# Four reorderings on the vector and scalar engines of a streaming encoder: the norm's reciprocal, the unit copies, a join, and the priority of two sums

## The chip, the cores and the metric

One Trainium2 chip, one core of it. The time is the device time of one launch in microseconds (us). A core has a matrix engine (TensorE, PE in the rows, with its weight loads as PEld), VectorE (DVE), ScalarE (ACT), GpSimd (POOL) and SyncE (SP); POOL and SP issue the transfers here. The products of TensorE collect in banks of PSUM, which VectorE and ScalarE read out in this kernel.

## The reference

Two layers over 512 prompt rows and 8 x 16 sample rows (640 columns in the kernel), width 1024, in float32. Of each layer:

```
x += 1/2 * SwiGLU_1(RMSNorm(x))                      w_gu: 1024 -> 2 x 2816, w_down: 2816 -> 1024
h  = RMSNorm(x)
z  = h @ w_in      columns: conv B | C | V | q | k | v | gates
y_c = B * causal_depthwise_conv3(C * V)              512 channels
y_a = chunk-band attention, 8 heads x 64
m  = sigmoid(g_c) * (y_c @ w_conv_out) + sigmoid(g_a) * (y_a @ w_attn_out);  x += m @ w_o
x += 1/2 * SwiGLU_2(RMSNorm(x))
```

and a last RMSNorm. Keys, values and the convolution's state are outputs too.

## The kernel before, in words

Activations stand with the width on the partitions: 8 tiles `x` of 128 x 640. Every product is made in three parts: an operand is split into a rounded high part (`hi`, a cast on ScalarE) and the rest (`lo`, a subtraction on VectorE), and TensorE multiplies hi·hi, hi·lo and lo·hi. So each weight slab of 128 x 1024 comes in by SyncE as `raw` (3 buffers), is cast to `whi` by ScalarE (L305) and gives `wlo` on VectorE (L310); 3 buffers each.

Most products use seven multiplications of half blocks in place of eight (`seven`, `gate_up`, `down_rows`, `gate_pair`, `unit`): the 640 columns stand as two halves of 320, and sums of weights and of operands are formed ahead. Their names are X11, X21, XN6, XT5, XT7, X22, XT4, and they are made in that order, 12 matmuls of 128 x 320 each. Products collect in three banks `pa`, `pb`, `pc` (in a unit two pairs, `A` and `B`, and `C`): `pa` takes X11, then XN6 on top, XT7 on top, XT4 on top; after each step a copy or a sum reads the bank out before the next step adds to it. Four slabs (s0 to s3) feed one such group; for a group of kind `gu` VectorE also makes the weight sum `s65` (lines 270 and 271, two half sums, recorded as L249 like every `add`), for kind `mix` the sum `s6`.

How the slabs come: `slabs` is the list of all weights in order of use. `load` issues the transfer, `source` makes a slab's sum, `prep` calls `source` and casts, and puts the lo part into `pending`; `flush` issues the pending lo parts. `slab` takes the next slab and prepares the one two places on; `quiet` takes it and prepares nothing; `ahead` calls `source` for the slab after the prepared ones.

Three engines keep the order that the code is written in within blocks called `manual_schedule` (PE, DVE and ACT); in the middle of a feed-forward only PE does (from the gate after `free`), and a scheduler orders DVE and ACT there. `soon()` gives what stands inside it a higher priority with that scheduler.

The places that the change touches:

- `gate_up`, branch `first` (L756 on): the first gate of a feed-forward. Where the norm is `new` (three feed-forwards: b of layer 0, a and b of layer 1) it makes, between the products, the sum of squares (`ex.total`, five matmuls into `nps`), the root on ScalarE (`ex.root`, L585), the weight sum (`source`), the reciprocal (L589) and a diagonal of it in `ssum` (L482) by `ex.diagonal`, and spreads it over the partitions by four matmuls `nbc` (L595). Then comes XT4 into `pa`.
- `gate_up`, the other branch: the gates after it. `add(g, pa, c5)` empties `pa` ahead of XT4, `add(u, pc, u2)` empties `pc`. `add` is L249.
- `unit` (L1411 on) multiplies 8 tiles of y by 4 x 8 blocks of `w_conv_out` (`co`, twice: m0 = 0 and 4) or `w_attn_out` (`ao`, twice). After XT4 a scalar copy reads `A` out (L1435). The two units of a kind use the same two banks, with A and B exchanged.
- The table `at(place, i, jobs)` in `outputs` says which jobs are done at which spot of which gate pair or unit: `scale` and `bend` (a gate's norm and its sigmoid, L1132), `weigh`, `join` (products with the gates, L1309), `give` and `gave` (hi and lo part of the merged m, L1497 and L1504).
- Behind the last unit, `ao4`, come the products `po` with `w_o` (L372), in `mixer`: `po` 0 and `po` 1 use the banks of the unit, `po` 2 two halves `po_2a` and `po_2b`, and each has a slab of its own.

Of the kernel before, what the change touches and what calls it, by code (L numbers as in the profile page):

```python
# [10 lines left out]
F32 = mybir.dt.float32  # L11
# [169 lines left out]
def trunk(ctx: ExitStack, tc: tile.TileContext, xin, wst, small, pbias, samplebias, kcache, vcache,  # L181
# [66 lines left out]
    def add(out, a, b):  # L248
        DVE.tensor_tensor(out=out, in0=a, in1=b, op=ALU.add)  # L249
# [2 lines left out]
    whole = slice(0, CH)  # L252
    sources = {}

    def source(i):

        if i >= len(slabs):
            return None
        if i not in sources:
            kind, n, arg = slabs[i]  # L260
            ra = load(n)
            if kind == "plain":
                sources[i] = [(ra, slice(0, arg))]
            elif arg == 0:
                sources[i] = [(ra, whole)]
            else:
                rb = load(n + 1)
                if arg == 1 and kind == "gu":
                    st = sums[n] = pool[0].tile([P, CH], F32, tag="s65", name=f"s65_{n}", bufs=1)
                    add(st[:, h2], rb[:, h1], rb[:, h2])  # L270
                    add(st[:, h1], st[:, h2], ra[:, h1])
                    sources[i] = [(st, whole)]
                elif arg == 1:

                    flush()
                    st = sums[n] = spool[0].tile([P, CH // 2], F32, tag="s6", name=f"s6_{n}", bufs=1)
                    add(ra[:, h1], ra[:, h1], rb[:, h1])
                    add(st, ra[:, h1], rb[:, h2])
                    add(rb[:, h1], rb[:, h1], rb[:, h2])
                    sources[i] = [(st, h1), (rb, h1)]  # L280
                elif arg == 2:
                    if kind == "gu":
                        add(ra[:, h1], ra[:, h1], rb[:, h1])
                    add(ra[:, h2], sums.pop(n)[:, h1], ra[:, h2])
                    sources[i] = [(ra, whole)]
                else:
                    sources[i] = [(rb, h2)]
        return sources[i]
# [26 lines left out]
    def slab(hold=False):  # L315

        flush()
        i = used[0]
        used[0] += 1
        while len(ready) < min(i + 2, len(slabs)):  # L320
            prep(len(ready))
            flush()
        prep(i + 2)
        if not hold:
            flush()
        return ready[i], slabs[i]
# [414 lines left out]
    def gate_up(fp, n, ex, first, tails, put, j, pair, later, at):  # L741

        pa, pb, pc = (att(f"p{i}{n}")[:, :HT] for i in "abc")

        def mul(ps, s, half, x, ks, start, stop):
            block(ps, s, half, lambda kp: tuple(z[:, x] for z in ex.ops[kp]), ks, start, stop)

        def spot(name):
            step(later, f"g{at}{name}")

        every, most, end = range(NP), range(NP - 1), range(NP - 1, NP)
        g, u = tmp(f"g{n}"), tmp(f"u{n}")
        t1, t2 = slice(0, HT), slice(HT, T)
        c1, u2, c5 = u[:, t1], u[:, t2], g[:, t2]
        rho = ex.rho
        if first:  # L756

            new = not ex.known
            s0, s1 = quiet(), quiet()
            mul(pa, s0, 0, X11, every, True, True)  # L760
            ACT.copy(c1, pa)
            if ex.rest:
                ex.rest()
            prep(used[0])
            flush()
            for t in tails[:2]:
                t()
            mul(pc, s1, 1, XT5, every, True, True)
            ACT.copy(c5, pc)
            if new:  # L770
                ACT.activation(ex.sq, x[KT - 1], AF.Square)
                ex.add()
                mul(pb, s0, 1, X21, most, True, True)
                mul(pa, s1, 0, XN6, most, False, True)
                mul(pb, s0, 1, X21, end, True, True)
                mul(pa, s1, 0, XN6, end, False, True)
            else:
                mul(pa, s1, 0, XN6, every, False, True)
                mul(pb, s0, 1, X21, every, True, True)
            ACT.copy(u2, pa)  # L780
            add(u[:, t1], pb, c1)
            for t in tails[2:]:
                t()
            tails.clear()
            s2 = quiet()
            prep(len(ready))
            flush()

            def third():
                mul(pc, s2, 1, X22, every, False, True)  # L790
                add(u[:, t2], pc, u2)

            if new:
                third()
                ex.total(acc(f"nps{n}")[:, 0])
                ex.root()
                source(len(ready) + 1)
                ex.diagonal()
                prep(len(ready))
            mul(pa, s2, 0, XT7, every, False, True)  # L800
            add(g[:, t2], pa, c5)
            flush()
            if new:
                nbc = acc(f"nbc{n}")
                ex.spread([nbc[:, a, :HT] for a in range(2)])
            DVE.tensor_tensor(out=g[:, t2], in0=g[:, t2], in1=rho[:, t2], op=ALU.mult)
            if not new:
                third()
                prep(len(ready))
                flush()  # L810
            s3 = slab(True)[0]
        else:
            s0 = quiet()
            mul(pa, s0, 0, X11, every, True, True)
            with soon():
                ACT.copy(c1, pa)
            prep(used[0] + 1)
            spot("e1")
            held = [t() for t in tails]
            tails.clear()  # L820
            spot("e2")
            flush()
            mul(pb, s0, 1, X21, every, True, True)
            s1 = slab(True)[0]
            flush()
            mul(pa, s1, 0, XN6, every, False, True)
            with soon():
                ACT.copy(u2, pa)
            cb = fp.tile([P, 2, HT], F32, tag="cap", name=f"cb{n}", bufs=5)[:, 0]
            ACT.copy(cb, pb)  # L830
            POOL.dma_start(u[:, t1], cb, accum_op=ALU.add)
            for t in held:
                t()
            spot("e3")
            mul(pc, s1, 1, XT5, every, True, True)
            with soon():
                ACT.copy(c5, pc)
            s2 = slab(True)[0]
            spot("e4")
            mul(pa, s2, 0, XT7, every, False, True)  # L840
            add(g[:, t2], pa, c5)
            DVE.tensor_tensor(out=g[:, t2], in0=g[:, t2], in1=rho[:, t2], op=ALU.mult)
            flush()
            ahead()
            mul(pc, s2, 1, X22, every, False, True)
            add(u[:, t2], pc, u2)
            s3 = slab(True)[0]
            ahead()
        mul(pa, s3, 0, XT4, every, False, True)
        DVE.tensor_tensor(out=g[:, t1], in0=pa, in1=rho[:, t1], op=ALU.mult)  # L850
        if first:
            ahead()
        ACT.activation(g, g, AF.Silu, scale=-1.0)
        spot("e7")
        flush()

        def tail(weights=True):

            if weights:
                begin()  # L860
            DVE.tensor_tensor(out=g, in0=g, in1=rho, op=ALU.mult)
            hi = hp.tile([P, T], F32R, tag="hhi", name=f"ahi{n}")
            lo = hp.tile([P, T], F32R, tag="hlo", name=f"alo{n}")
            if pair:
                parts = pair.product(n, u, g, hi, lo)
            else:
                DVE.tensor_tensor(out=u, in0=u, in1=g, op=ALU.mult)
                parts = lambda: split(hi, lo, u)
            flush()
            if weights:  # L870
                ahead()
            else:
                parts()
            put(j, (hi, lo))
            return parts

        tails.append(tail)
# [409 lines left out]
    def outputs(l, gp, X, st, cs, yc, yas, sigmoid, gates):  # L1287
# [123 lines left out]
        def unit(name, m0, to, last=False):  # L1411
# [53 lines left out]
                add(rows(0, t2)[:, i], C[i], rows(0, t2)[:, i])  # L1465
            if last:
                add(rows(1, t2), rows(1, t2), z)
            s3 = slab(True)[0]
            ahead()
            mul(a, s3, 0, XT4, False)  # L1470
            copy(rows(1, t1), -1.0)
            flush()
            spot(me, 5)

        def weigh(*ms):
            def job():
# [42 lines left out]
        at("co0", 1, scale(4))  # L1519
        at("co0", 2, bend(4))  # L1520
        at("co0", 3, scale(6))
        at("co0", 5, bend(6))
        at("co4", 2, weigh(0, 1))
        at("co4", 5, weigh(2, 3))
        at("g8", 1, second.opening)
        at("g8", 2, second.firsts)
        at("g8", 3, second.raw_low(0))
# [7 lines left out]
        at("g12", 3, scale(10))  # L1535
        at("g12", 4, bend(8))
        at("ao0", 3, scale(12))
        at("ao0", 5, bend(10), join(0))
        at("g14", 1, join(2))
        at("g14", 2, join(1))  # L1540
        at("g14", 3, join(3))
# [1 line left out]
        at("ao4", 2, give(0, 1))  # L1543
        at("ao4", 3, gave(0, 1))
        at("ao4", 4, give(2, 3))
        at("ao4", 5, gave(2, 3))
        for m in (2, 4, 6):
            gate_pair(m)

# [576 lines left out]
```

## Time and profile before

| | |
|---|---|
| three runs | 2495.89, 2496.51, 2498.94 us, median 2496.51 |
| the profiled execution | 2496.66 us, its span 2494.7 us |
| granted clock of TensorE, mean | 0.998 |
| ScalarE busy | 1450.0 us, 58% |
| VectorE busy | 2119.2 us, 85% |
| transferred | 308.10 MB, mean 124 GB/s |

The page has the busy time of each engine, then the waits. A row of the timeline reads: start in us from the beginning of the span, length in us, engine, line of the kernel, operation, output<-inputs by the program's names, sizes, number, and in brackets the idle time ahead of it with what ended it. Matmuls overlap: one begins every 0.147 us and its record is 0.31 us long.

### The profile page before, as it was taken

How to read it: one execution, taken by the hardware profiler on the slowest of the kernel's cores; microseconds unless marked ns; L12 is line 12 of the kernel's file. 1: busy time of each engine (PE TensorE's matmuls, PEld its weight loads, DVE VectorE, ACT ScalarE, POOL GpSimd, SP SyncE). 2: the span in 40 equal slices, each digit the busy share in tenths (PEclk: the TensorE clock that was granted, in tenths of full speed). 3: DMA queues.
4: the chain of work that ended last, by engine and by line, in shares of the span. 5: the costliest groups of instructions: out<-in, count | busy, mean ns of one | idle time of the engine just before them, and what ended most of it. 6: DMA issues, size and time to landing. Idle time of an engine off the chain costs nothing.

```text
span 2494.7 us, 43515 instructions
## 1 busy us (share of the span) xinstructions
PE 2478.1 (99%) x17048; PEld 2419.0 (97%) x17048; DVE 2119.2 (85%) x3322; ACT 1450.0 (58%) x2343; POOL 370.7 (15%) x445
## 2 busy tenths in 40 slices
PE   9999999999999999999999999999999999999998
PEld 8999999888999999999999999998899999999998
DVE  7888888878888899888798889888788888989887
ACT  7455556674666555555565555556646665555554
POOL 0011211211111011111001111221111110111111
PEclk9999999999999999999999999999999999999999
DMA  4245665335345344655435555643344553455554
GB/s 146 82 107 124 138 135 130 106 115 167 99 119 145 101 116 118 138 135 135 117 90 126 129 134 123 138 119 115 125 153 104 126 141 95 119 133 122 129 135 110
DMA packets 133261, 308.10 MB, mean 124 GB/s; under 512 B 12768, under 2 KB 76128, under 8 KB 133056
## 3 DMA queue, kind: packets, MB, share of 16 engines
q1 hardware_dynamic: 68976, 219.18, 27.3%
q0 software_dynamic: 63360, 85.50, 20.6%
q8 instruction: 133, 2.18, 0.4%
q10 hardware_dynamic: 720, 0.65, 0.1%
q14 instruction: 72, 0.59, 0.1%
HBM read 221.13 MB, written 7.94 MB: 92 GB/s over the span
## 4 chain that ended last, share of the span: by engine, by line
PE 94%; DVE 3%; ACT 2%; DMA 1%; issue 0%; SPq 0%; DVEq 0%; ACTq 0%
PE pab L395 12%; PE paa L395 11%; PE pcb L395 6%; PE pca L395 6%; PE daa L962 5%; PE dab L962 5%; PE po L372 4%; PE qa L395 4%; PE pbb L395 3%; PE pba L395 3%; PE dca L962 3%; PE dcb L962 3%; PE pda L372 2%; PE pv L1622 2%; PE ma_cv L395 2%; PE qc L395 2%
## 5 line engine op out<-in xcount | busy, mean ns | idle before, releaser
L310 DVE TENSOR_TENSOR wlo<-raw,whi 128x512 fp32r<-128x512 f32 (+1 forms) x583 | 598.6, 1030 | 236.1 <-ACT whi L305 230.6
L305 ACT CAST whi<-raw 128x512 fp32r<-128x512 f32 (+1 forms) x583 | 519.9, 897 | 348.0 <-PE pbb L395 44.6
L305 ACT CAST whi<-s 128x1024 fp32r<-128x1024 f32 (+1 forms) x164 | 153.6, 937 | 248.1 <-issue 107.8
L395 PE MATMUL pab<-xhib,whi 128*128 128x320 f32 x704 | 218.3, 310 | 0.4 <-DVE gb L249 0.4
L395 PE MATMUL pab<-xhib,wlo 128*128 128x320 f32 x704 | 217.4, 309 | 0.0
L395 PE MATMUL pab<-xlob,whi 128*128 128x320 f32 x704 | 217.4, 309 | 0.0
L395 PE MATMUL paa<-xhia,whi 128*128 128x320 f32 x640 | 198.0, 309 | 0.2 <-DVE ga L249 0.2
L395 PE MATMUL paa<-xloa,whi 128*128 128x320 f32 x640 | 197.6, 309 | 0.0
L395 PE MATMUL paa<-xhia,wlo 128*128 128x320 f32 x640 | 197.6, 309 | 0.0
L310 DVE TENSOR_TENSOR wlo<-s,whi 128x1024 fp32r<-128x1024 f32 (+1 forms) x164 | 176.6, 1077 | 10.4 <-ACT whi L305 10.4
L395 PEld LDWEIGHTS pab<-xhib,whi 128*128 128x128 f32 x704 | 132.2, 188 | 1.1 <-DVE gb L249 0.9
L395 PEld LDWEIGHTS pab<-xlob,whi 128*128 128x128 f32 x704 | 132.2, 188 | 0.2
L395 PEld LDWEIGHTS pab<-xhib,wlo 128*128 128x128 f32 x704 | 132.2, 188 | 0.0
L395 PEld LDWEIGHTS paa<-xhia,whi 128*128 128x128 f32 x640 | 120.2, 188 | 0.5 <-DVE ga L249 0.5
L395 PEld LDWEIGHTS paa<-xloa,whi 128*128 128x128 f32 x640 | 120.2, 188 | 0.1
L395 PEld LDWEIGHTS paa<-xhia,wlo 128*128 128x128 f32 x640 | 120.2, 188 | 0.0
L249 DVE TENSOR_TENSOR raw<-raw,raw 128x512 f32<-128x512 f32 x164 | 112.2, 684 | 1.8 <-DMA raw<-in_wst 0.2
L249 DVE TENSOR_TENSOR raw<-s,raw 128x512 f32<-128x512 f32 x164 | 112.3, 685 | 0.0
L395 PE MATMUL pcb<-xhib,whi 128*128 128x320 f32 x352 | 108.7, 309 | 0.0
L395 PE MATMUL pcb<-xlob,whi 128*128 128x320 f32 x352 | 108.7, 309 | 0.0
L395 PE MATMUL pcb<-xhib,wlo 128*128 128x320 f32 x352 | 108.7, 309 | 0.0
L986 POOL DMA_DIRECT2D x<-c_b x52 | 62.6, 1203 | 309.5 <-ACT c_b L979 134.5
(816 smaller groups left out, 8170.8 us busy)
## 6 DMA issues: line engine op xcount, KB each, us to landing
raw<-in_wst SPq DMA_DIRECT2D x375, 512.0 KB, 3.7
x<-c_b POOLq DMA_DIRECT2D x52, 320.0 KB, 5.1
x<-c_a POOLq DMA_DIRECT2D x50, 320.0 KB, 5.0
kc<-in_kcache SPq DMA_DIRECT2D x32, 256.0 KB, 4.1
vc<-in_vcache SPq DMA_DIRECT2D x16, 512.0 KB, 4.5
ub<-cbb POOLq DMA_DIRECT2D x42, 160.0 KB, 5.9
ua<-cba POOLq DMA_DIRECT2D x38, 160.0 KB, 5.4
x<-u_a POOLq DMA_DIRECT2D x18, 320.0 KB, 5.1
```

Source lines behind the costliest of these rows:

```text
L249: DVE.tensor_tensor(out=out, in0=a, in1=b, op=ALU.add)
L305: ACT.copy(hi[:, d], src[:, c])
L310: DVE.tensor_tensor(out=lo, in0=src, in1=hi.bitcast(F32), op=ALU.subtract)
L372: PE.matmul(ps[a] if isinstance(ps, list) else ps[:, a, :HT], w, x[:, a * HT : (a + 1) * HT], start=first and j == 0, stop=last and j == 2)
L395: PE.matmul(ps, a, b, start=start and kp == 0 and j == 0, stop=stop and kp == NP - 1 and j == 2, skip_group_check=True)
L962: PE.matmul(ps[u], w, y, start=start and i == 0 and j == 0, stop=i == 1 and j == 2, skip_group_check=True)
L986: POOL.dma_start(rows(r, cols), z, accum_op=ALU.add)
L1622: PE.matmul(pv[t], xx[:, t * P : (t + 1) * P], w[:, kk * AW : (kk + 1) * AW], start=c == 0 and kk == 0 and j == 0, stop=c == KT // 2 - 1 a ...
```

## The change

Four things, in three functions and the table:

- A new function `start` makes the first half of a weight sum `s65`. The first gate calls it ahead of `ex.diagonal`, and `source`, which makes the sum, comes behind. `source` calls `start` too.
- In the later gates the two sums that empty `pa` and `pc` get the higher priority.
- In `unit`, the slab of XT4 is taken by `quiet`, and the casts of the slab after it are issued behind the copy that reads `A` out, not ahead of it. A new spot 6 stands behind the lo parts, spot 5 ahead of them.
- In the table, `bend(6)` moves from the end of `co0` to the end of `co4`, `weigh(2, 3)`, `bend(10)` and `gave(2, 3)` move to spot 6, and `join(0)` stays at spot 5, now ahead of the lo parts.

```diff
+    started = {}
+
+    def start(i):
+
+        if i in sources or i >= len(slabs) or slabs[i][0] != "gu" or slabs[i][2] != 1:
+            return
+        n = slabs[i][1]
+        load(n)
+        rb = load(n + 1)
+        st = started[i] = pool[0].tile([P, CH], F32, tag="s65", name=f"s65_{n}", bufs=1)
+        add(st[:, h2], rb[:, h1], rb[:, h2])
+
     def source(i):
...
                 if arg == 1 and kind == "gu":
-                    st = sums[n] = pool[0].tile([P, CH], F32, tag="s65", name=f"s65_{n}", bufs=1)
-                    add(st[:, h2], rb[:, h1], rb[:, h2])
+                    start(i)
+                    st = sums[n] = started.pop(i)
                     add(st[:, h1], st[:, h2], ra[:, h1])
                     sources[i] = [(st, whole)]
...
                 ex.root()
+                start(len(ready) + 1)
+                ex.diagonal()
                 source(len(ready) + 1)
-                ex.diagonal()
                 prep(len(ready))
...
             mul(pa, s2, 0, XT7, every, False, True)
-            add(g[:, t2], pa, c5)
+            with soon():
+                add(g[:, t2], pa, c5)
...
             mul(pc, s2, 1, X22, every, False, True)
-            add(u[:, t2], pc, u2)
+            with soon():
+                add(u[:, t2], pc, u2)
...
-            s3 = slab(True)[0]
-            ahead()
+            flush()
+            s3 = quiet()
             mul(a, s3, 0, XT4, False)
             copy(rows(1, t1), -1.0)
+            prep(used[0] + 1)
+            ahead()
+            spot(me, 5)
             flush()
-            spot(me, 5)
+            spot(me, 6)
...
-        at("co0", 5, bend(6))
         at("co4", 2, weigh(0, 1))
-        at("co4", 5, weigh(2, 3))
+        at("co4", 6, weigh(2, 3), bend(6))
...
-        at("ao0", 5, bend(10), join(0))
+        at("ao0", 5, join(0))
+        at("ao0", 6, bend(10))
...
-        at("ao4", 5, gave(2, 3))
+        at("ao4", 6, gave(2, 3))
```

TensorE, SyncE and GpSimd have the same rows in the same order as before. Three places where VectorE or ScalarE has another order (the changed kernel's own line numbers are up to 18 higher):

VectorE at the first gate of the second feed-forward of layer 0, from the sum that empties `pcb` on; `s` is the weight sum, `ninvb` the reciprocal, `ssumb` the diagonal. Before:

```order
L249 TENSOR_TENSOR ub_0_9181<-pcb_0_9179,ub_0_9181 128x320
L249 TENSOR_TENSOR s_124_9270<-raw_9268 128x512
L249 TENSOR_TENSOR s_124_9270<-s_124_9270,raw_9266 128x512
L589 RECIPROCAL ninvb_8634<-nrmsb_8633 128x5
L482 TENSOR_TENSOR ssumb_8635<-ident,ninvb_8634 128x640
L249 TENSOR_TENSOR gb_0_9180<-pab_0_9177,gb_0_9180 128x320
```

And in the changed kernel:

```order
L249 TENSOR_TENSOR ub_0_9181<-pcb_0_9179,ub_0_9181 128x320
L249 TENSOR_TENSOR s_124_9270<-raw_9268 128x512
L601 RECIPROCAL ninvb_8634<-nrmsb_8633 128x5
L494 TENSOR_TENSOR ssumb_8635<-ident,ninvb_8634 128x640
L249 TENSOR_TENSOR s_124_9274<-raw_9268 128x512
L249 TENSOR_TENSOR s_124_9274<-s_124_9274,raw_9266 128x512
L249 TENSOR_TENSOR gb_0_9180<-pab_0_9177,gb_0_9180 128x320
```

The reciprocal and the diagonal have moved ahead of the second half sum, and the first half sum stands there twice, once for each call of `start`.

VectorE at the fourth gate of the same feed-forward, from the lo part of a weight on; `gb_3` is the sum that empties `pab`, `alob_2` the lo part of the third gate's result. Before:

```order
L310 TENSOR_TENSOR wlo_9676<-raw_9630,whi_9675 128x1024
L911 TENSOR_TENSOR alob_2_9624<-deb_2_9625,ahib_2_9623 128x640
L249 TENSOR_TENSOR gb_3_9601<-pab_3_9598,gb_3_9601 128x320
L249 TENSOR_TENSOR ub_3_9602<-pcb_3_9600,ub_3_9602 128x320
L842 TENSOR_TENSOR gb_3_9601<-gb_3_9601,rhob_8636 128x320
```

And in the changed kernel:

```order
L322 TENSOR_TENSOR wlo_9678<-raw_9632,whi_9677 128x1024
L249 TENSOR_TENSOR gb_3_9603<-pab_3_9600,gb_3_9603 128x320
L926 TENSOR_TENSOR alob_2_9626<-deb_2_9627,ahib_2_9625 128x640
L249 TENSOR_TENSOR ub_3_9604<-pcb_3_9602,ub_3_9604 128x320
L856 TENSOR_TENSOR gb_3_9603<-gb_3_9603,rhob_8636 128x320
```

The sum has moved one place forward, ahead of the lo part.

ScalarE at the end of the unit `ao4` of layer 0, from the hi part of m's third tile on; `aao_4` is the unit's bank A, the two `whi` are the slabs of `po` 1 and `po` 2. Before:

```order
L1497 CAST m_2hi<-yc_4682 128x640
L1497 CAST m_3hi<-yc_4682 128x640
L305 CAST whi_8577<-raw_8560 128x1024
L305 CAST whi_8643<-raw_8580 128x1024
L1435 ACTIVATE ya_4623<-aao_4_8462 128x2x320
L1497 CAST m_4hi<-mm_7138 128x640
```

And in the changed kernel:

```order
L1515 CAST m_2hi<-yc_4682 128x640
L1515 CAST m_3hi<-yc_4682 128x640
L1450 ACTIVATE ya_4623<-aao_4_8462 128x2x320
L317 CAST whi_8590<-raw_8560 128x1024
L317 CAST whi_8643<-raw_8593 128x1024
L1515 CAST m_4hi<-mm_7138 128x640
```

The copy has moved ahead of both casts. VectorE's order at this place is unchanged.

## The prediction

> **What bounds the kernel now.** I read the page first (busy time by engine), then the list of who waited for whom on TensorE, then the timeline at each place where TensorE waits near a line of the change. TensorE decides:
>
> ```profile
> PE 2478.1 (99%) x17048; PEld 2419.0 (97%) x17048; DVE 2119.2 (85%) x3322; ACT 1450.0 (58%) x2343; POOL 370.7 (15%) x445
> PE pab L395 <- DVE gb L249: 0.4, 2, 0.2
> PE paa L395 <- DVE ga L249: 0.2, 1, 0.2
> ```
>
> TensorE is busy for all but 16.6 us of the 2494.7 us span, so the change can give little: it adds and removes no matmul. The last two rows name one wait that three feed-forward layers share (twice `pab`, once `paa`). The records hide part of a wait in the matmul before it, so I measure waits by start to start: in a dense run one 128x320 matmul follows the other after 0.147 us. Whatever is over that is a wait. After a wait the first matmul is also long (0.41 to 0.42 us where others take 0.31), so each wait costs 0.11 us more: the **restart**.
>
> The order of instructions on TensorE, SyncE and GpSimd is unchanged. Only VectorE and ScalarE rows move, so for each place I ask when the row that TensorE waits for now ends.
>
> **First gate of a feed-forward (3 times).** VectorE's rows, ScalarE's root, and TensorE's:
>
> ```profile
> 846.67 0.69 DVE L249 TENSOR_TENSOR s<-s,raw 128x512 f32<-128x512 f32 x1
> 847.28 0.18 DVE L589 RECIPROCAL ninvb<-nrmsb 128x5 f32<-128x5 f32 x1
> 847.57 0.82 DVE L482 TENSOR_TENSOR ssumb<-ident,ninvb 128x640 f32<-128x640 f32 x1
> 848.43 0.49 DVE L249 TENSOR_TENSOR gb<-pab,gb 128x320 f32<-128x320 f32 x1
> 846.55 0.27 ACT L585 ACTIVATE nrmsb<-npsb,epst 128x5 f32<-128x5 f32 x1 [0.52 <-PE npsb L472]
> 848.08 0.31 PE L395 MATMUL pab<-xhib,wlo 128*128 128x320 f32 x1
> 848.45 1.34 PE L595 MATMUL nbcb<-ssumb,ones 128*128 128x320 f32 x4
> 849.78 0.31 PE L395 MATMUL pab<-xlob,whi 128*128 128x320 f32 x1
> ```
>
> The broadcast `nbcb` could start at 848.23 (848.08 + 0.147) and starts at 848.45, behind `ssumb`: 0.22 us of wait and 0.11 of restart. The root ends at 846.82, so with the reciprocal ahead of the second half sum, `ssumb` starts at 847.16 (root, 0.05 to the other engine, 0.29 between the two rows) and ends at 847.98: this wait goes, -0.33 us.
>
> But the half sum ahead of it is not kept. `source` calls `start` again, `start` looks only into `sources`, so the first half sum is **done twice** (the order shows the row twice, and VectorE has three rows more in the program). Behind `ssumb` now stand the repeated half (847.89), the second half (848.58) and only then the add `gb<-pab`, at 849.19 with the 0.61 between a half sum and the next row. It ends at 849.68. The last product of the gate (XT4) adds into the same bank, so it must wait for that add: first matmul at 849.73, the second, with the restart, at 849.99. Before it stood at 849.78. So **+0.21 us each, +0.63** in all. Bounds: -0.33 each if the add were in time, +0.7 each if the add slipped by one more half sum.
>
> **Fourth gate (3 times).** This is the wait of the rows quoted first:
>
> ```profile
> 885.67 0.82 DVE L911 TENSOR_TENSOR alob<-deb,ahib 128x640 fp32r<-128x640 f32 x1
> 886.40 0.48 DVE L249 TENSOR_TENSOR gb<-pab,gb 128x320 f32<-128x320 f32 x1
> 886.45 0.31 PE L395 MATMUL pcb<-xhib,wlo 128*128 128x320 f32 x1
> 886.94 0.41 PE L395 MATMUL pab<-xhib,whi 128*128 128x320 f32 x1 [0.19 <-DVE gb L249]
> ```
>
> XT4 could start at 886.60 and starts at 886.94: 0.34 + 0.11 = 0.45 us. With the higher priority the add comes ahead of `alob` and takes its place, 885.67 to 886.15, 0.4 us before TensorE needs it. **-0.45 each, -1.35.** Bounds: -1.35 to 0. The other gates whose rows are reordered have no wait before; their rows are the same ones within a few places, and I price them at nothing: XT4's adds move forward there, and the casts that move back belong to the next gate, some four products (7 us) away. If that cover failed, one cast is 1.05 us.
>
> **Conv output products (per layer).** ScalarE, then TensorE:
>
> ```profile
> 692.27 0.62 ACT L305 CAST whi<-s 128x512 fp32r<-128x512 f32 x1 [2.21 <-PE aco L1428]
> 693.32 0.70 ACT L1435 ACTIVATE yc<-aco 128x640 f32<-128x640 f32 x1
> 693.92 1.54 ACT L1132 ACTIVATE gt<-gt,sm 128x640 f32<-128x640 f32 x2
> 695.36 0.69 ACT L1435 ACTIVATE mm<-aco 128x640 f32<-128x640 f32 x1
> 693.70 0.30 PE L1428 MATMUL aco<-xhi,wlo 128*128 128x320 f32 x1
> 694.07 0.42 PE L1428 MATMUL bco<-xhi,whi 128*128 128x320 f32 x1
> 696.10 0.41 PE L1428 MATMUL aco<-xhi,whi 128*128 128x320 f32 x1
> ```
>
> `bco` needs the bank that the copy at 693.32 empties: 0.22 of wait. Twelve matmuls and a restart later (695.94) `aco` needs the copy at 695.36, which stood behind two sigmoids: 0.16. With two restarts 0.60 us. Both copies now come earlier (692.27, and about 694.0), so this goes: **-1.2** for two layers, which I take as alike. The two casts now behind the copy end at 694.0, and VectorE's rows for them do not start sooner before either.
>
> The sigmoids reappear at the end of `co4`, ahead of the next gate's first copy:
>
> ```profile
> 706.97 0.43 ACT L1329 COPY g<-qa 128x320 f32<-128x320 f32 x1 [1.06 <-PE qa L395]
> 710.65 0.42 ACT L1337 COPY g<-qa 128x320 f32<-128x320 f32 x1
> 758.29 0.41 PE L395 MATMUL qa<-thi,whi 128*128 128x320 f32 x1
> 757.81 0.43 ACT L1329 COPY g<-qa 128x320 f32<-128x320 f32 x1 [0.73 <-DVE ya L1309]
> ```
>
> Counted from the end of XT4's last matmul, ScalarE now does the copy (0.60 to the next row), two casts (1.05), two sigmoids (1.44) and the gate's copy (0.43): with 0.05 at both ends 3.6 us. TensorE needs that copy after 24 matmuls, less the 0.16 by which a record ends after the next start: 3.36. A **new wait** of 0.25 + 0.11. The gate's second copy ends 4.1 us after the first one starts (710.65 + 0.42 - 706.97), 24 further matmuls take 3.52: some 0.05 + 0.11 more. Together +0.5 per layer, **+1.0**; bounds 0 to +1.2.
>
> The attention output unit `ao0` has the same chain ahead of gate 14, whose copy at 757.81 also waited for the join (`ya`, L1309). The join now stands ahead of the lo parts, but the casts stand behind the copy. The wait before was 0.30 (758.29 against 757.99), by the chain it is 0.25: **-0.05**.
>
> **Attention output unit `ao4` and the products behind it.** The largest term:
>
> ```profile
> 778.52 1.05 ACT L305 CAST whi<-raw 128x1024 fp32r<-128x1024 f32 x1 [0.37 <-DVE ya L249]
> 781.04 0.69 ACT L1435 ACTIVATE ya<-aao 128x640 f32<-128x640 f32 x1
> 779.60 1.22 DVE L310 TENSOR_TENSOR wlo<-raw,whi 128x1024 fp32r<-128x1024 f32 x1 [0.42 <-ACT whi L305]
> 780.75 0.82 DVE L1504 TENSOR_TENSOR m_2lo<-yc,m_2hi 128x640 fp32r<-128x640 f32 x1
> 782.22 0.81 DVE L1309 TENSOR_TENSOR ya<-ya,gt 128x640 f32<-128x640 f32 x1
> 782.95 1.22 DVE L310 TENSOR_TENSOR wlo<-raw,whi 128x1024 fp32r<-128x1024 f32 x1
> 779.38 0.31 PE L1428 MATMUL aao<-xhi,wlo 128*128 128x320 f32 x1
> 781.78 0.56 PE L372 MATMUL po<-m_0hi,whi 128*128 128x320 f32 x2 [0.34 <-ACT ya L1435]
> 784.23 0.41 PE L372 MATMUL po_2a<-m_0hi,wlo 128*128 128x320 f32 x1
> 2012.49 0.31 PE L1428 MATMUL aao<-xhi,wlo 128*128 128x320 f32 x1
> 2016.86 0.42 PE L372 MATMUL po_2a<-m_0hi,wlo 128*128 128x320 f32 x1
> ```
>
> Here the unit copy `ya<-aao` goes ahead of **two** casts, and these feed the very next products: `po` 1 uses the first, `po` 2 the second. In the first layer that ends the wait at 781.78 (0.5 us). But the first cast, which started at 778.52, now starts behind a copy that must wait for XT4's end (779.69). Step by step: copy 779.72, cast 780.32 to 781.37, its lo part on VectorE 781.41, `m_2lo` 1.15 later (782.56), `m_3lo` and `ya<-ya,gt` (1.47 between their first and the row behind) 784.03, the second lo part 0.73 later, 784.76 to 785.98. VectorE's rows stand in the same order as before, so all of them are queued behind the late one. The matmul that needs the second lo part, at 784.23 before, starts at 786.03: **+1.80**. Earlier waits of `po` 1 (for the cast, then its lo part) lie inside this, and so does the 0.5 us that is saved.
>
> The chain takes 6.34 us from XT4's end. In the second layer that is 2012.80 + 6.34 = 2019.14 against 2016.86: **+2.28**. Together **+4.08**. Later rows of VectorE (`m_4` to `m_7`) move by as much as TensorE does, so their distance stays. Bounds: -0.6 if the casts were in time, +4.1 with the chain as it stands; I take the chain, because no row in it is unknown.
>
> **Sum.** +0.63 - 1.35 - 1.2 + 1.0 - 0.05 + 4.08 = +3.1 us. The profiled execution took 2496.66 us (span 2494.7); with +3.1 it is 2499.8. It stood 0.15 above the median of the three runs (2496.51), so I predict **2499.6 us**, 0.12% up.
>
> **Rivals.**
>
> *The change does what its words say*: the repeated half sum hides, or is not run, and the adds are in time at the first gates. That is -0.33 three times in place of +0.63: 2498.0 us. For it: the wait at 848.45 is real and goes. Against: the add would have to end by about 849.3, and I find 849.68. Chance 0.10.
>
> *The casts cost nothing*, because something I don't see lets VectorE reach the second lo part in time at `po`. Then only -0.6 remains of that term: 3.1 - 4.08 - 0.6 = -1.6, 2495.0 us. Against: six rows of known length in a fixed order. Chance 0.08.
>
> *The clock drops*, the slower side. The trace shows the granted clock fall once while the program runs:
>
> ```profile
> 6.00:9.00 3.00, 3.00 (x12) 2.88 (x12) 2.23 (x5) 2.29 (x4) 0.00 (x0) 1.00 1.04 381
> 2485.00:2487.00 2.00, 0.61 (x4) 0.52 (x4) 1.97 (x6) 0.68 (x2) 0.00 (x0) 1.00 0.79 282
> 2487.00:2495.00 8.00, 1.22 (x2) 0.50 (x2) 4.54 (x11) 0.00 (x0) 0.00 (x0) 0.50 0.68 233
> ```
>
> With TensorE busy for 0.61 of 2 us, the clock is 0.50 from then on. At `po` TensorE now waits some 2.2 us out of 4.7, the longest piece 1.5. If that is enough, the matmuls behind run slowly for a while: the first window shows such a slow stretch at the program's start, 12 matmuls in 3 us where 20 go at full pace, so 8 x 0.147 = 1.2 us are lost each time, 2.4 in two layers: 2502.1 us, 0.23% slower than before. [...] Chance 0.10.
>
> [...]
>
> **How the numbers follow.** Forecast 0.72, with 2498.3 to 2501.2 as its own range (the two uncertain small terms, and 1 us for the spread of runs). Range for 8 in 10: down past the first rival, up past the clock: 2496.0 to 2502.5; the second rival's 0.08 and some tails are left out. 0.2% is 5 us, about what a measurement of this kernel can tell from no change: faster by more 0.02 (all gains and no new wait would give only -4), slower by more 0.13 (the clock, and tails), within 0.85.
>
> **What would show it.** In the changed profile: TensorE's first `po_2a<-m_0hi,wlo` some 6.3 us after the last `aao` record ends, released by VectorE's `wlo`; no wait at the fourth gate; `nbcb` following `pab` at once, and XT4 then waiting for `gb`; ScalarE's `g<-qa` of gate 8 behind two sigmoids, and TensorE waiting for it. I am wrong if `po` runs without a wait, or if the clock column leaves 1.00 there.

## The result, and the profile after

| | before | after |
|---|---|---|
| median of 22 runs each | 2496.56 us | 2500.06 us (2499.41 to 2501.1) |
| ratio, 95% interval | | 1.0013 (1.0007 to 1.0019) |
| span of the profiled execution | 2494.7 us | 2497.9 us |
| granted clock, mean | 0.998 | 0.999 |

The change costs 3.5 us, 0.13%; 2499.6 was predicted. The page and the list of who waited for whom on TensorE, of the changed kernel (total us, times, longest us):

```profile
PE 2477.4 (99%) x17048; PEld 2419.2 (97%) x17048; DVE 2120.7 (85%) x3325; ACT 1448.9 (58%) x2343; POOL 370.7 (15%) x445
```

```profile
PE po_2a L384 <- DVE wlo L322: 2.6, 2, 1.3
PE po L384 <- DVE wlo L322: 0.8, 2, 0.4
PE pab L407 <- DVE gb L249: 0.8, 2, 0.4
PE paa L407 <- DVE ga L249: 0.4, 1, 0.4
```

VectorE has its three rows more (3325 against 3322). The first two rows are new and stand at `po`. The last two carry the names of the wait before at the fourth gate, but belong to another place: the first gate, and 0.4 us long in place of 0.2. A row of this list names two tiles, not a place in the program.

**Where the time went.** TensorE has the same matmuls in the same order in both traces, so each one has a partner. I take the start of each after minus before; what this difference grows by across a stretch is what the change costs there.

| stretch | predicted, us | layer or feed-forward: measured, us | sum |
|---|---|---|---|
| `co0` and `co4` | -1.2 | -0.58, -0.62 | -1.20 |
| gate 8 | +1.0 | +0.47, +0.47 | +0.94 |
| gates 10 to 14, `ao0` | -0.05 | +0.16, +0.12 | +0.28 |
| `ao4` and `po` | +4.08 | +1.78, +2.26 | +4.04 |
| first gates | +0.63 | +0.29, +0.30, +0.30 | +0.89 |
| fourth gates | -1.35 | -0.45, -0.46, -0.46 | -1.37 |
| together | +3.1 | | +3.58 |

The start of the program (-0.18) and the last norm (-0.26) differ too; the change touches neither, and both moved by a few tenths from one execution to the next in the other runs as well.

**`ao4` and `po`**, layer 1 of the changed kernel: XT4's last matmul, the copy and the casts on ScalarE, VectorE's rows, and the matmul that waits at the end.

```profile
2013.79 0.31 PE L1443 MATMUL aao<-xhi,wlo 128*128 128x320 f32 x1
2014.13 0.71 ACT L1450 ACTIVATE ya<-aao 128x640 f32<-128x640 f32 x1 [1.57 <-PE aao L1443]
2014.73 1.98 ACT L317 CAST whi<-raw 128x1024 fp32r<-128x1024 f32 x2
2015.80 1.22 DVE L322 TENSOR_TENSOR wlo<-raw,whi 128x1024 fp32r<-128x1024 f32 x1 [2.21 <-ACT whi L317]
...
2018.41 0.82 DVE L1324 TENSOR_TENSOR ya<-ya,gt 128x640 f32<-128x640 f32 x1
2019.15 1.22 DVE L322 TENSOR_TENSOR wlo<-raw,whi 128x1024 fp32r<-128x1024 f32 x1
2017.08 0.56 PE L384 MATMUL po<-m_0hi,wlo 128*128 128x320 f32 x2 [0.41 <-DVE wlo L322]
2020.42 0.42 PE L384 MATMUL po_2a<-m_0hi,wlo 128*128 128x320 f32 x1 [1.32 <-DVE wlo L322]
```

ScalarE was idle for 1.57 us before the copy, while the first cast could have run (before the change it ran there). From XT4's end (2014.10) to the matmul at 2020.42 it is 6.32 us; 6.34 was predicted. VectorE waits 2.21 us for the first cast and then runs without a gap to the second lo part.

**The first gate** of feed-forward b, layer 0:

```profile
848.80 0.82 DVE L494 TENSOR_TENSOR ssumb<-ident,ninvb 128x640 f32<-128x640 f32 x1
849.54 0.68 DVE L249 TENSOR_TENSOR s<-raw 128x512 f32<-128x512 f32 x1
850.26 0.69 DVE L249 TENSOR_TENSOR s<-s,raw 128x512 f32<-128x512 f32 x1
850.87 0.48 DVE L249 TENSOR_TENSOR gb<-pab,gb 128x320 f32<-128x320 f32 x1
849.74 0.31 PE L407 MATMUL pab<-xhib,wlo 128*128 128x320 f32 x1
849.88 1.24 PE L607 MATMUL nbcb<-ssumb,ones 128*128 128x320 f32 x4
851.50 0.39 PE L407 MATMUL pab<-xhib,whi 128*128 128x320 f32 x1 [0.38 <-DVE gb L249]
851.72 0.31 PE L407 MATMUL pab<-xlob,whi 128*128 128x320 f32 x1
```

`nbcb` follows `pab` after 0.14 us: the wait before is gone. The repeated half sum (849.54) pushes the add to 850.87, and XT4 waits for its end.

**The fourth gate** of the same feed-forward:

```profile
887.49 0.48 DVE L249 TENSOR_TENSOR gb<-pab,gb 128x320 f32<-128x320 f32 x1
888.39 0.31 PE L407 MATMUL pcb<-xhib,wlo 128*128 128x320 f32 x1
888.54 0.31 PE L407 MATMUL pab<-xhib,whi 128*128 128x320 f32 x1
```

The add ends at 887.97, 0.57 us before XT4, which now follows at 0.15.

**The conv units and gate 8**, layer 0; the two sigmoids and gate 8's copy on ScalarE, then TensorE at both places:

```profile
706.07 1.55 ACT L1147 ACTIVATE gt<-gt,sm 128x640 f32<-128x640 f32 x2
707.52 0.41 ACT L1344 COPY g<-qa 128x320 f32<-128x320 f32 x1
693.53 0.31 PE L1443 MATMUL aco<-xhi,wlo 128*128 128x320 f32 x1
693.67 0.31 PE L1443 MATMUL bco<-xhi,whi 128*128 128x320 f32 x1
707.61 0.31 PE L407 MATMUL qb<-hhim,wlo 128*128 128x320 f32 x1
707.98 0.42 PE L407 MATMUL qa<-thi,whi 128*128 128x320 f32 x1
```

`bco` no longer waits. At gate 8 TensorE waits 0.22 us (707.98 against 707.61 + 0.147) for the copy that ends at 707.93.

**Gate 12**, which no term of the prediction had. Before, then after, layer 0: VectorE at gate 8, a lo part that waits for ScalarE's cast and then the row that reads out XT4, and some 15 us later TensorE at gate 12, with ScalarE's copy that it waits for in the second.

```profile
710.78 0.69 DVE L310 TENSOR_TENSOR wlo<-raw,whi 128x512 fp32r<-128x512 f32 x1 [0.95 <-ACT whi L305]
717.52 0.49 DVE L1353 TENSOR_TENSOR g<-qa,rrm 128x320 f32<-128x320 f32 x1 [0.52 <-PE qa L395]
732.99 0.31 PE L395 MATMUL qb<-hhim,wlo 128*128 128x320 f32 x1
733.26 0.42 PE L395 MATMUL qa<-thi,whi 128*128 128x320 f32 x1
```

```profile
711.31 0.69 DVE L322 TENSOR_TENSOR wlo<-raw,whi 128x512 fp32r<-128x512 f32 x1 [1.18 <-ACT whi L317]
717.44 0.48 DVE L1368 TENSOR_TENSOR g<-qa,rrm 128x320 f32<-128x320 f32 x1
732.70 0.41 ACT L1344 COPY gt<-qa 128x320 f32<-128x320 f32 x1
732.75 0.31 PE L407 MATMUL qb<-hhim,wlo 128*128 128x320 f32 x1
733.16 0.41 PE L407 MATMUL qa<-thi,whi 128*128 128x320 f32 x1
```

Before, VectorE waited 0.52 us for TensorE ahead of the second row. After, its lo part comes 0.53 us later, because the cast does (711.31 against 710.78), and no idle time is left ahead of the second row. Fifteen us on, TensorE is 0.24 us earlier than before (732.75 against 732.99), VectorE's readout was only 0.08, and the wait at gate 12 grows from 0.12 to 0.26 us.

**The clock** at `po`, layer 1, in two windows (start and end, length, busy us of PE, PEld, DVE, ACT and POOL with their rows, granted clock, DMA share, GB/s):

```profile
2016.00:2018.00 2.00, 1.59 (x10) 1.33 (x11) 2.00 (x3) 0.72 (x1) 0.00 (x0) 1.00 0.00 0
2018.00:2020.00 2.00, 1.10 (x8) 0.84 (x6) 2.00 (x3) 0.00 (x0) 0.00 (x0) 1.00 0.85 262
```

TensorE is busy for 2.69 of 4 us, and the clock stays at 1.00.

### The profile page after: what moved, and what is told of

Same layout as the page of the kernel before. It is cut to its first block, busy times and chain, and to the rows that moved or that the text cites. A ratio compares the mean times of both kernels' runs of the same rounds, so it can differ in the third digit from the quotient of the medians.

```text
span 2497.9 us, 43514 instructions
## 1 busy us (share of the span) xinstructions
PE 2477.4 (99%) x17048; PEld 2419.2 (97%) x17048; DVE 2120.7 (85%) x3325; ACT 1448.9 (58%) x2343; POOL 370.7 (15%) x445
## 4 chain that ended last, share of the span: by engine, by line
PE 93%; DVE 3%; ACT 2%; issue 1%; DMA 1%; SPq 0%; DVEq 0%; ACTq 0%
PE pab L407 12%; PE paa L407 11%; PE pcb L407 6%; PE pca L407 6%; PE daa L977 5%; PE dab L977 5%; PE po L384 4%; PE pbb L407 3%; PE pba L407 3%; PE qa L407 3%; PE dcb L977 3%; PE dca L977 3%; PE pda L384 2%; PE pv L1640 2%; PE ma_cv L407 2%; PE poa L384 2%
```

## The experiments

Each kernel was timed against the kernel before on one chip. The before medians of the three sets were 2496.51 (e1 to e4), 2496.94 (e6 to e9) and 2496.64 us (e5, e10). The intervals reach about 2 us to either side, so the steps in the traces, found as in the table above, carry the finer statements.

### e1: in ao4 alone, the casts ahead of the copy again

```diff
-            flush()
-            s3 = quiet()
+            if last:
+                s3 = slab(True)[0]
+                ahead()
+            else:
+                flush()
+                s3 = quiet()
...
-            prep(used[0] + 1)
-            ahead()
+            if not last:
+                prep(used[0] + 1)
+                ahead()
```

> The changed kernel, but in the unit ao4 alone the two weight casts stand ahead of the copy that reads bank A out, as before the change; the spots and all other units stay changed. Theory (ScalarE's late casts make the two waits at po): the steps of +1.8 us (layer 0) and +2.3 us (layer 1) at po go, so the time is 2500.1 - 4.0 = 2496.0 us, ratio to the kernel before about 0.9998, and the first po_2a<-m_0hi,wlo starts some 4.5 us after the last aao record ends in place of 6.3. Rival (the casts cost nothing, the 3.5 us stand elsewhere): 2500 us, ratio 1.0014. Rival (something downstream of po waits anyway, so that only part comes back): 2498 us.

Measured: 2496.19 us, ratio 0.9998 (0.9989 to 1.0007). In the trace the steps at `po` against the changed kernel are -2.00 and -2.27 us, together -4.3. The largest term of the sum stands, and nothing behind `po` takes it back. Layer 0 gives back 0.2 us more than the change took: before the change `po` 1 waited 0.50 us there, for a copy behind a cast whose weights came late (ScalarE waits 0.51 us for the transfer, at 780.08). In e1 that wait is 0.28 us.

### e4: the kernel before, with the copy ahead of the casts in ao4 alone

```diff
-            s3 = slab(True)[0]
-            ahead()
+            if last:
+                flush()
+                s3 = quiet()
+            else:
+                s3 = slab(True)[0]
+                ahead()
             mul(a, s3, 0, XT4, False)
             copy(rows(1, t1), -1.0)
+            if last:
+                prep(used[0] + 1)
+                ahead()
```

> The kernel before, with one thing changed: in the unit ao4 the copy that reads bank A out stands ahead of the two weight casts. Theory: this alone costs +4.0 us (+1.8 in layer 0, +2.3 in layer 1): 2496.5 + 4.0 = 2500.6 us, ratio to the kernel before 1.0016. Rival (the loss needs the other parts of the change): +0 to +2 us. Rival (only the first wait in layer 0 goes, the casts are in time): -0.6 us, 2495.9 us.

Measured: 2500.38 us, ratio 1.0016 (1.0007 to 1.0025). The steps at `po` are +1.79 and +2.26 us. So this edit costs the same with and without the rest of the change.

### e7: one cast ahead of the copy, one behind it

```diff
+            if last:
+                s3 = slab(True)[0]
+                ahead()
...
             mul(a, s3, 0, XT4, False)
+            if last:
+                flush()
             copy(rows(1, t1), -1.0)
-            prep(used[0] + 1)
-            ahead()
+            if last:
+                begin()
+            else:
+                prep(used[0] + 1)
+                ahead()
             spot(me, 5)
-            flush()
+            if not last:
+                flush()
```

> The changed kernel, but in ao4 the first of the two casts stands ahead of the copy and the second behind it. Theory (the first cast starts VectorE's chain, the second is not on it): the whole 4.0 us come back although po 1 no longer waits for the copy, because po_2a waits for VectorE's second lo part, whose end is set by the first cast: 2496.0 us, ratio 0.9998. Rival (each cast behind the copy costs its length): about half comes back, 2498 us. Rival (the saved 0.5 us of po 1 in layer 0 is kept): 2495.4 us.

Measured: 2496.03 us, ratio 0.9995 (0.9986 to 1.0004). The second cast is not on the path: with it alone behind the copy the 4 us come back. In layer 1 the trace shows the rest of the theory. Against the kernel before, the 0.10 us that `po` 1 saves are lost again at `po_2a`, which starts when VectorE's second lo part ends (2016.17 + 1.22 = 2017.39):

```profile
2016.17 1.22 DVE L322 TENSOR_TENSOR wlo<-raw,whi 128x1024 fp32r<-128x1024 f32 x1
2017.45 0.41 PE L384 MATMUL po_2a<-m_0hi,wlo 128*128 128x320 f32 x1
```

In layer 0 the profiled execution (2497.35 us, the longest of the eleven) can't tell, because the first cast had to wait for its weights there:

```profile
779.36 1.05 ACT L317 CAST whi<-raw 128x1024 fp32r<-128x1024 f32 x1 [0.86 <-DMA raw<-in_wst]
```

Whether the 0.5 us of layer 0 is kept when the weights come in time (the third rival, 2495.4 us) stays open: the interval holds both.

### e2: the first half sum made once

```diff
-        if i in sources or i >= len(slabs) or slabs[i][0] != "gu" or slabs[i][2] != 1:
+        if i in sources or i in started or i >= len(slabs) or slabs[i][0] != "gu" or slabs[i][2] != 1:
```

> The changed kernel, but the first half of the weight sum at the three first gates is made once (VectorE has three rows less). Theory (the repeated half sum, 0.69 us, holds the add that XT4 waits for): the wait at XT4 goes and nothing comes in its place, each first gate goes from +0.29 to -0.33 us against before, together -1.9 us: 2498.2 us, ratio to the kernel before 1.0006. Rival (the second half sum alone, now behind the diagonal, is late enough): the wait at XT4 gets shorter by the 0.3 us only, 2499.2 us, ratio 1.0010. Rival (the repeat is hidden and XT4 waits for another row): 2500.1 us.

Measured: 2498.53 us, ratio 1.0006 (0.9998 to 1.0015). The add comes out in time and XT4 follows the four broadcasts at 0.89 us (0.94 before, 1.62 in the changed kernel):

```profile
850.33 0.48 DVE L249 TENSOR_TENSOR gb<-pab,gb 128x320 f32<-128x320 f32 x1
850.07 1.24 PE L607 MATMUL nbcb<-ssumb,ones 128*128 128x320 f32 x4
850.96 0.49 PE L407 MATMUL pab<-xhib,whi 128*128 128x320 f32 x1
```

The steps are -0.62, -0.64 and -0.61 us, 1.87 in all; 0.28 us of it were lost in this execution at the attention of layer 1, where the kernels have the same rows. Both other rivals fall: the wait goes wholly, and the repeat was its cause.

### e3: the two sigmoids in co4, not at its end

```diff
-        at("co4", 6, weigh(2, 3), bend(6))
+        at("co4", 4, bend(6))
+        at("co4", 6, weigh(2, 3))
```

> The changed kernel, but the two sigmoids of bend(6) stand behind the fourth product of co4, where ScalarE was idle for 1.7 us, not at the unit's end. Theory: the waits at gate 8 (0.33 and 0.15 us per layer) go, and with them the growth at gate 12 that I did not predict (0.16 to 0.23 us per layer), since VectorE's rows of gate 8 are no longer 0.5 us late: -1.2 us for two layers, 2498.9 us, ratio to the kernel before 1.0009. Rival (VectorE's own chain sets gate 12, whatever the sigmoids do): gate 8 gives 0.9 us and gate 12 takes about 0.7 of it back, 2499.8 us. Rival (the sigmoids now hold the copy of XT4's bank in co4): a new wait there of up to 0.3 us per layer.

Measured: 2498.77 us, ratio 1.0009 (1.0 to 1.0017). From gate 8 to gate 12 the two layers gain 0.65 us each, 1.3 together, of it 0.19 and 0.23 at gate 12:

```profile
704.26 0.70 ACT L1450 ACTIVATE mm<-aco 128x640 f32<-128x640 f32 x1 [1.38 <-PE aco L1443]
716.60 0.49 DVE L1368 TENSOR_TENSOR g<-qa,rrm 128x320 f32<-128x320 f32 x1 [0.56 <-PE qa L407]
```

The sigmoids (701.34 to 702.88) lie in idle time now: ScalarE waits 1.38 us behind them for the unit's last product. VectorE has its 0.56 us of reserve back at the end of gate 8. So the growth at gate 12 came from the sigmoids, and was no limit of VectorE's own.

### e5: the kernel before, with the priority alone

```diff
-            add(g[:, t2], pa, c5)
+            with soon():
+                add(g[:, t2], pa, c5)
...
-            add(u[:, t2], pc, u2)
+            with soon():
+                add(u[:, t2], pc, u2)
```

> The kernel before, with the higher priority of the two sums that empty banks and nothing else. Theory: the wait at the fourth gate of three feed-forwards goes and no other place moves: -1.37 us, ratio to the kernel before 0.9995; in the trace three steps of -0.35 and -0.11 us. Rival (the rows that move back, casts and lo parts of the next gates, make a wait of their own): part of it comes back, 0 to -1 us.

Measured: 2495.32 us, ratio 0.9995 (0.9986 to 1.0004). Three steps of -0.44 to -0.46 us at the fourth gates, 1.35 in all, and none at the other gates. One more of about -0.3 us stands at `po` 1 of layer 0, which this edit doesn't touch: the weights came earlier, and the wait is 0.17 us there in place of 0.50.

### e6: the three losses undone at once

The edits of e1, e2 and e3 together.

> The changed kernel with the three losses undone at once: casts ahead of the copy in ao4, the first half sum made once, the sigmoids of bend(6) behind co4's fourth product. What stays of the change: the reciprocal ahead of the second half sum, the priority of the two sums, copies ahead of casts in the other units. Theory (the terms add, since each is a wait of TensorE in another stretch): 2500.1 - 4.0 - 1.9 - 1.4 = 2492.8 us, ratio to the kernel before 0.9985. Rival (when TensorE arrives earlier, VectorE or a transfer is the next to be late, in another place): 2494 to 2495 us.

Measured: 2493.28 us, ratio 0.9985 (0.9976 to 0.9994), faster than both kernels. Against before the trace shows -0.59 and -0.60 us at the conv units, -0.31 to -0.33 at each of the three first gates and -0.46 at each fourth gate. The terms add: the ratio is the one expected. This execution also had the shorter wait at `po` 1 of layer 0, as in e5 (-0.33), and lost 0.27 us at the attention of layer 1, as e2 did; the edits touch neither.

### e8: the second lo part directly behind the first

As e6, but in `ao4` the first cast, the copy and the second cast in this order, so that the `flush` behind spot 5 issues both lo parts, ahead of those of m:

```diff
             mul(a, s3, 0, XT4, False)
             copy(rows(1, t1), -1.0)
-            if not last:
+            if last:
+                begin()
+            else:
                 prep(used[0] + 1)
                 ahead()
```

> As the kernel with the three losses undone, but in ao4 the first cast, then the copy, then the second cast, and on VectorE the lo part of the second slab directly behind that of the first, ahead of the lo parts of m and of ya*gt. Theory (the chain copy, cast, lo parts, ya*gt, second lo part is what po waits for): with the second lo part 2.2 us earlier none of the po waits is left, and the waits of the kernel before at this place go too (0.6 + 0.1 us in layer 0, 0.1 + 0.1 in layer 1): 2492.8 - 0.9 = 2491.9 us, ratio 0.9982. Rival (m_2's lo part, now later, makes a new wait in the second block of po): 2492.8 us or more.

Measured: 2492.49 us, ratio 0.9982 (0.9973 to 0.9991). Against e6 the steps at `po` are -0.37 and -0.23 us, and no later wait comes in their place. This is the best of the versions; its lead over e6 is read from the traces, since the two intervals overlap.

### e10: the copy made twice

```diff
             copy(rows(1, t1), -1.0)
+            if last:
+                copy(rows(1, t1), -1.0)
```

> The changed kernel, but the copy that reads bank A out in ao4 is made twice, so that both casts start 0.60 us later. Theory (the chain behind XT4 moves as a whole): +0.6 us in each layer, 2500.1 + 1.2 = 2501.3 us, ratio to the kernel before 1.0019; po 1 waits about 0.75 us, its first lo part 0.56 and po_2a 1.47, 2.8 us in 5.3, and the clock stays at 1.00. Rival (2.8 us of waits in 5.3 are enough for the clock to fall, as 1.9 us in one piece with two shorter ones were in the kernel with a third cast): the clock column leaves 1.00 behind po 1, and the first layer loses some 0.4 us more.

Measured: 2501.6 us, ratio 1.002 (1.0011 to 1.0029). The steps are +0.76 and +0.75 us: the second copy costs ScalarE 0.74 (1.34 to the cast's start, less 0.60), and the chain moves by just about that.

```profile
2014.77 1.44 ACT L1450 ACTIVATE ya<-aao 128x640 f32<-128x640 f32 x2 [1.57 <-PE aao L1443]
2016.11 1.98 ACT L317 CAST whi<-raw 128x1024 fp32r<-128x1024 f32 x2
2017.19 0.56 PE L384 MATMUL po<-m_0hi,whi 128*128 128x320 f32 x2 [0.70 <-ACT whi L317]
2020.00:2022.00 2.00, 0.68 (x5) 0.42 (x4) 2.00 (x3) 0.00 (x0) 0.00 (x0) 1.00 0.53 207
```

By start to start TensorE waits 0.86, 0.57 and 1.48 us within 5.5 us, and the clock stays at 1.00.

### e9: a third cast behind the copy

```diff
             prep(used[0] + 1)
+            if last:
+                ACT.copy(ready[-1][0], sources[len(ready) - 1][0][0])
             ahead()
```

> The changed kernel with one more cast behind the copy in ao4: the first of the two is made twice, so that its lo part waits for the second time. Theory (every cast behind the copy moves VectorE's whole chain by its 0.95 us from one row to the next): the first po_2a<-m_0hi,wlo starts 0.95 us later in each layer, 2500.1 + 1.9 = 2502.0 us, ratio 1.0022, and the granted clock stays 1.00 there. Rival (the clock falls when TensorE waits some 3.2 of 5.7 us): a slow stretch follows, 2503.2 us or more, and the clock column leaves 1.00. Rival (the casts are not on the path): 2500.1 us.

Measured: 2504.65 us, ratio 1.0029 (1.0018 to 1.004). My number missed, for two reasons. The scheduler put the second slab's cast ahead of the repeated one, so both stand ahead of the first lo part and the chain grows by 1.88 us a layer (2017.79 to 2019.67), not 0.95. And the clock fell. Layer 1, ScalarE's casts, `po` 1 and the windows:

```profile
2017.79 1.98 ACT L317 CAST whi<-raw 128x1024 fp32r<-128x1024 f32 x2
2019.67 1.04 ACT L1489 CAST whi<-raw 128x1024 fp32r<-128x1024 f32 x1
2020.77 0.56 PE L384 MATMUL po<-m_0hi,whi 128*128 128x320 f32 x2 [1.85 <-ACT whi L1489]
2020.00:2022.00 2.00, 0.85 (x4) 0.58 (x4) 1.25 (x2) 0.72 (x1) 0.00 (x0) 0.91 0.00 0
2022.00:2024.00 2.00, 1.97 (x7) 1.97 (x8) 2.00 (x3) 0.00 (x0) 0.00 (x0) 0.50 0.38 115
2024.00:2026.00 2.00, 2.00 (x10) 1.78 (x10) 2.00 (x4) 0.00 (x0) 0.00 (x0) 0.73 0.37 147
```

`po` 1 waits 2.02 us in one piece in each layer. Worked out from the mean clock of the windows (0.51 from 786 to 788 and 0.64 from 788 to 790 in layer 0; 0.91, 0.50 and 0.73 in layer 1, above), the clock falls to 0.50 about 2.1 us after this wait ends in layer 0 (at 783.88) and about 0.9 us after it in layer 1 (at 2020.77), and stays there for some 3.4 us, in which a matmul follows the other after 0.267 us in place of 0.147. Layer 0 loses 2.3 us against the changed kernel, 0.4 more than the chain. Layer 1 loses 1.9, the chain alone: TensorE's slow matmuls end only when the second lo part is there anyway. In two of the six executions the mean clock is 0.999 (0.997 in the profiled one), as in kernels without such a fall, so the fall does not seem to come every time.

## Why the prediction was right, and where it was off

**`ao4` and `po`, +4.08: right.** +1.78 and +2.26 us against +1.80 and +2.28. e1 takes it out, e4 makes it alone, e10 moves it by the length that it adds. e7 shows which cast it is: the first one, because VectorE's rows stand queued behind its lo part. In layer 0 the close agreement holds for one execution: the prediction was read from the same trace of the kernel before, in which `po` 1 waited 0.50 us. With the 0.17 us of e5 there, the same change would have cost about 2.1 us.

**Fourth gates, -1.35: right.** -1.37 in the change, -1.35 alone in e5. The cover for the rows that move back held.

**Conv units, -1.2, and gate 8, +1.0: right.** -1.20 and +0.94. No run has the conv units alone; e6 keeps their steps (-0.59 and -0.60), and e3 takes gate 8's away.

**First gates, +0.63: right in kind, +0.89 in size.** I let XT4 start 0.05 us behind the add's end; in layer 0 it started 0.15 behind it (851.50 against 850.87 + 0.48), and the other two steps are as large. e2 shows the cause, and gives -0.33 a gate when the sum is made once, as the first rival priced it.

**Gate 12: missed, +0.38.** The step that failed is the moved sigmoids. I priced them by the one copy that TensorE waits for next, and left out what else stands behind them on ScalarE: the cast of the next slab, on whose end VectorE's rows of gate 8 wait. They came 0.5 us late (711.31 against 710.78), which used up VectorE's reserve of 0.52 us (the row at 717.52). From there VectorE and ScalarE, which wait for each other's sums and casts in turn, set the pace to gate 12: both were only 0.1 us earlier than before, and so was the copy that TensorE waits for. That the sigmoids are the cause is shown by e3; the path between gate 8 and gate 12 is read from the trace alone. Part of it was hidden by `ao0`, which came out as -0.07 and -0.03: its -0.05 had been counted once, though the unit stands in both layers.

**The sum** was +3.1, the steps give +3.58, the medians +3.5. The two missed sizes, 0.26 and 0.38, make up the difference, less 0.17 by which the other terms together came out lower.

**The rivals.** "What its words say" is e2, 2498.5 us where 2498.0 was given: it needs a kernel that does not repeat the sum. "The casts cost nothing" is excluded by e1 and e4. "The clock drops" did not happen in the change, but did one step further on: in e9 the clock went to 0.50 at the same place, with a wait of 2.0 us where the change has 1.5. I had put its cost at 1.2 us a layer; it was 0.4 and nothing, since most of the slow stretch lies under a wait.

## What to carry to other kernels

When a copy that frees a bank is put ahead of a cast, ask first whether the copy could run yet: it waited 1.57 us for TensorE here, and both casts queued behind it on ScalarE waited too, then VectorE, 2.21 us for the first of them. When a job is moved to another spot, follow every row that stands behind it there, not only the next one that the bottleneck waits for, and look how much reserve (idle time with the bottleneck named as its end) the second engine has. Where the bottleneck's order is the same in two traces, the difference of start times, matmul by matmul, tells each step to some 0.05 us, when the intervals of whole runs reach 2 us to either side here. But it compares two executions: where a transfer is waited for, as at `po` 1 of layer 0, the same code gave waits of 0.17 to 0.50 us.

## What the runs showed of the hardware that was not expected

The clock fell where I had expected it to stay at 1.00: in e9 no wait at `po` was longer than 2.02 us, and yet it went to 0.50 in both layers, for some 3.4 us each time. e10, with 1.48 us as its longest wait in layer 1, keeps 1.00, and so does the changed kernel with 1.47 in layer 0. Layer 0 of e9:

```profile
782.00:784.00 2.00, 0.14 (x2) 0.12 (x2) 0.14 (x1) 1.83 (x2) 0.00 (x0) 1.00 0.00 0
784.00:786.00 2.00, 1.59 (x10) 1.33 (x11) 2.00 (x3) 0.00 (x0) 0.00 (x0) 1.00 0.00 0
786.00:788.00 2.00, 2.00 (x8) 1.59 (x7) 2.00 (x3) 0.00 (x0) 0.00 (x0) 0.51 0.74 262
788.00:790.00 2.00, 1.51 (x7) 1.51 (x8) 2.00 (x4) 0.79 (x2) 0.00 (x0) 0.64 0.23 43
```

TensorE is busy for 1.73 us of the 4 ahead of this fall (782 to 786), and in layer 1 for 1.77 of the 4 in whose last part the clock falls (2018 to 2022: 0.92 and 0.85). In the emptiest two neighbouring windows at `po` it is busy for 2.27 us in e10 (2018 to 2022: 1.59 and 0.68) as in the changed kernel (782 to 786, the same two numbers), and the clock stays at 1.00. The longest wait (2.02 us in e9 against 1.48 and 1.47) sorts these cases the same way. What the fall depends on, and from which value, is not shown.

Of two equal copies of 128x640 out of a bank, one behind the other into the same tile, the second added 0.74 us in e10 (1.34 from 2014.77 to the cast at 2016.11, less 0.60), where a copy followed by a cast took 0.60 (2014.13 to 2014.73 in the changed kernel).
